# Mixer chunks by channels: weights stationary, x normalised beforehand, squares summed by tokens, the scale by a GpSimd power

## The chip, the cores and the metric

The kernel runs on one core of a Trainium2 chip. The metric is the device time of one execution in microseconds, as a median of several runs. A core has five engines that work side by side, each through its own queue in order: TensorE (PE; its weight loads are shown as PEld), VectorE (DVE), ScalarE (ACT), GpSimd (POOL) and SyncE (SP), whose queue issues almost all DMAs here. Matmuls write PSUM, a small memory of banks of 128 partitions by 512 float32; everything else lies in SBUF.

## What is computed

Two layers over 256 tokens of 1024 channels, float32. Each layer is a half-step SwiGLU FFN, a token mixer, and another half-step FFN, every one between two RMS norms:

```python
for i in range(DEPTH):
    f = swiglu_ffn(rmsnorm(x, ffn1_norm_pre[i]), ffn1_w_in[i], ffn1_w_out[i])
    x = x + 0.5 * rmsnorm(f, ffn1_norm_post[i])

    h = rmsnorm(x, mix_norm_pre[i])
    p = h @ mix_w_in[i]
    qkv, z, beta_logit, a_logit, glu_in, gates = jnp.split(p, SPLITS, axis=-1)
    y_a = gated_deltanet(qkv, z, beta_logit, a_logit, ...)
    y_b = conformer_conv(glu_in, ...)
    g_a, g_b = jnp.split(jax.nn.sigmoid(gates), 2, axis=-1)
    y = (g_a * y_a + g_b * y_b) @ mix_w_out[i]
    x = x + rmsnorm(y, mix_norm_post[i])

    f = swiglu_ffn(rmsnorm(x, ffn2_norm_pre[i]), ffn2_w_in[i], ffn2_w_out[i])
    x = x + 0.5 * rmsnorm(f, ffn2_norm_post[i])
```

`gated_deltanet` runs a causal convolution of 4 taps and SiLU over q, k and v, makes q and k of unit length per head (8 heads of 128), forms decays from a cumulative sum, inverts a lower triangular matrix for each chunk of 64 tokens and scans over the chunks. `conformer_conv` gates half of its 2048 inputs by the sigmoid of the other half, runs a causal convolution of 31 taps per channel, a layer norm, SiLU and a projection.

## The kernel before

**Tiles.** The tokens are two blocks of 128 (`tb` 0 and 1). Every large product is done in three matmuls (`mm3`, lines 366 to 369): x and the weights are each split into a rounded part `hi` and the rest `lo`, and hi*hi, hi*lo and lo*hi are summed in PSUM. x is stationary (128 channels by 128 tokens), the weights move past it, 512 columns at a time.

**Weights.** `Stream` (lines 117 to 155) brings them in pieces of 128x1024: a DMA on SP into `raw` (three buffers), a copy on ACT into `whi` (line 146) and a subtraction into `wlo` (line 147) on DVE, or on POOL for the pieces of the mixer whose number is in the set `POOL`. `whi` and `wlo` have eight buffers each; a new piece is loaded when an old one is used up.

**Order.** PE's instructions run in the order in which the program writes them down. The other engines' order comes from a list scheduler, in which work written earlier goes first, moved by the offsets in `CFG` (`conv` back by 800, `ev` ahead by 1000 and so on). Side work that needs PE is woven in by `Lanes`: a job is a generator; `DELAY` gives the ticks from its adding to its first step and between its steps, `AFTER` the jobs that must have ended before. `tick` is called after every third of matmuls or so, 16 times in a chunk of 512 columns.

**The FFN** (`ffn`, line 446): 11 chunks of 512 columns, gated on eviction with the row scale `rstd`, transposed (line 464) and split again for the second product, whose results go through `post` (line 349): a Square with a sum on ACT, `rsqrt` (lines 237 to 256; for one column eleven small DVE instructions with the two before it), and an update of x (line 364). `pre` (line 271) then multiplies x by the norm's weights (line 277), transposes it (line 283), splits it (lines 260, 261) and computes the row scale r beside this (line 290). The scale is applied when results leave PSUM.

**The mixer** (`mixer`, line 484) runs through the 17 chunks of `PLAN` by `proj_in` (line 372). For each chunk and token block a PSUM bank (`mm`, four banks) receives tokens by 512 columns; `ev` copies it with the row scale into a staging tile (line 908). For the chunks of g, k, v and q, which are needed with channels on the partitions, `to_channels` (line 509) transposes the staging tile in blocks of 128x128 into PSUM (line 513, tag `tr`, three banks). `fin_glu` gates g; `conv4` (line 557) makes the four taps: an ACT copy with a scale (line 560), three DVE multiply-adds (line 562), SiLU on ACT. Beside this run:

- `conv31` (line 533), 31 taps over a pair of channel tiles on DVE (line 546), in one PSUM bank (`cacc`), the four pairs and the inverse one after the other
- `decays` (line 580): small DVE work on the `ka` chunk's first 16 columns, a cumulative sum on PE (lines 618 to 620), the sums out to DRAM and back as a broadcast (lines 632, 636), differences on DVE (line 639), Exp on ACT
- `k_tokens` and `q_tokens` (lines 659, 807): `squares` takes the squares of k or q on ACT (line 648), `sums` adds them over the channels by matmuls with a column of ones (line 656)
- `similarity` (matmuls on line 698), `inverse`, `merge`, and the scan
- `conv_norm` (line 975), the layer norm after the convolutions; its transposes (line 985) wait for the last of them (line 552)

Of the kernel before, what the change touches and what calls it, by code (L numbers as in the profile page):

```python
# [158 lines left out]
def trunk(ctx: ExitStack, tc: tile.TileContext, x_in, wfirst, consts, feat, pch, tokp,  # L159
# [49 lines left out]
    V.memset(ones, 1.0)  # L209
    warm = cpool.tile([P, 1], F32, name="warm")  # L210
# [46 lines left out]

    def split(hi, lo, src):

        S.copy(hi, src)  # L260
        V.tensor_tensor(lo, src, hi.bitcast(F32), op=ALU.subtract)  # L261
# [4 lines left out]

    def halves(tb):
        return [slots.tile([P, 2, 4, P], F32R, name="xt", tag=f"xt{tb}{hf}") for hf in range(2)]


    def pre(tb, wbc, xws):
        xw = slot(xws, [P, D], name="xw")
        xh = halves(tb)
        r = small(1, f"rstd{tb}")
        for hf in range(2):
            cs = slice(hf * 512, hf * 512 + 512)
            V.tensor_tensor(xw[:, cs], x[tb][:, cs], wbc[:, cs], op=ALU.mult)

        def steps():
            for hf in range(2):  # L280
                tr = ps_tr()
                for k in range(4):
                    T.transpose(tr[:, k, :], xw[:, hf * 512 + k * P: hf * 512 + (k + 1) * P], ident)
                with prio(tc, "pre"):
                    split(xh[hf][:, 0], xh[hf][:, 1], tr)
                if hf == 0:
                    yield
            with prio(tc, "stat"):
                ss = small(1, "ss")
                S.activation(xw, x[tb], AF.Square, accum_out=ss)  # L290
                V.tensor_scalar(ss, ss, 1.0 / D, RMS_EPS, op0=ALU.mult, op1=ALU.add)
                rsqrt(r, ss, 1)

        due[tb] = lanes.add(f"pre{tb}", steps())
        return xh, r


    def start():
# [14 lines left out]
        def stat(tb):  # L313
            jk = slot(15 + tb, [P, D], name="jk")
            ss = small(1, "ss")
            S.activation(jk, x[tb], AF.Square, accum_out=ss)
            V.tensor_scalar(ss, ss, 1.0 / D, RMS_EPS, op0=ALU.mult, op1=ALU.add)
            rsqrt(r[tb], ss, 1)
# [30 lines left out]
    def post(tb, acc, wbc, half, fws, jks):  # L349
        fw = slot(fws, [P, D], name="fw")  # L350
        jk = slot(jks, [P, D], name="jk")
        ss = small(2, "ss2")
        for hf in range(2):
            cs = slice(hf * 512, hf * 512 + 512)
            S.activation(jk[:, cs], acc[hf], AF.Square, accum_out=ss[:, hf:hf + 1])  # L355
            V.scalar_tensor_tensor(fw[:, cs], acc[hf], half, wbc[:, cs], op0=ALU.mult, op1=ALU.mult)  # L356
        s1 = small(1, "ss1")
        V.tensor_tensor(s1, ss[:, 0:1], ss[:, 1:2], op=ALU.add)
# [13 lines left out]
    def proj_in(xt, chunks, ev, fin, first=2):  # L372
# [111 lines left out]
    def mixer(xt, l, after_mix):  # L484
# [7 lines left out]
        rs = [xt[tb][1] for tb in range(2)]  # L492

# [3 lines left out]
        S.activation(aexp, tp[:, 0, :], AF.Exp)  # L497
# [24 lines left out]
        def fin_glu(c, stage):  # L522
            for i in range(2):
# [3 lines left out]
                tr = to_channels(stage, [i * P, 256 + i * P])  # L527
                sg = stt("sg")
                S.activation(sg, tr[:, 1, :], AF.Tanh, scale=0.5, bias=bgh[:, t:t + 1])
                S.activation(sg, sg, AF.Copy, scale=0.5, bias=0.5)  # L530
                V.scalar_tensor_tensor(h_of(t), tr[:, 0, :], pcc(C_BA, t), sg, op0=ALU.add, op1=ALU.mult)
# [48 lines left out]
        def decays():  # L580
# [10 lines left out]
            eo = small(32, "eo", bufs=1)  # L591
            S.activation(eo[:, 0:16], ba[:, 0].rearrange("p g b h -> p (g b h)"), AF.Exp, scale=-1.0)
# [32 lines left out]
            S.activation(ex, xin, AF.Exp)  # L625
            S.activation(neg_eg, ex[:, 0:16], AF.Copy, scale=-1.0)
# [6 lines left out]
            for gp in range(2):  # L633
# [7 lines left out]
                S.activation(dt, dt, AF.Exp)  # L641
                S.activation(gx[:, 4:8, :], gx[:, 4:8, :], AF.Exp)
# [3 lines left out]
        def squares(src, si):  # L646
            sq = slot(si, [P, 4, SEQ], name="sq")
            S.activation(sq, src, AF.Square)  # L648
            return sq

        def sums(sq):
            ps = ps_gd([P, 512])
            for tb in range(2):
                for hl in range(4):
                    th = tb * 4 + hl
                    T.matmul(ps[:, th:th + 1], sq[:, hl, tb * P:(tb + 1) * P], ones, start=True, stop=True)  # L656
            return ps

        def k_tokens(gp):
            sq = squares(kT[gp], 18 + gp)  # L660
            for tb in range(2):
                if tb:
                    yield
                tr = ps_tr()
                for hl in range(4):
                    T.transpose(tr[:, hl, :], kT[gp][:, hl, tb * P:(tb + 1) * P], ident)
# [3 lines left out]
            ps = sums(sq)  # L670
            V.tensor_scalar(ve, ps[:, 0:8], 1e-6, None, op0=ALU.add)
# [135 lines left out]
        def q_tokens(gp):  # L807
            sq = squares(qT[gp], 18 + gp)
            yield
            V.tensor_scalar(vq[:, gp * 8:gp * 8 + 8], sums(sq)[:, 0:8], float(P), P * 1e-6, op0=ALU.mult, op1=ALU.add)  # L810
# [79 lines left out]

        last = {}

        def ev(c, tb, ps):
            name, n = PLAN[c][0], chunks[c][0]
            if tb == 0:
# [5 lines left out]
            if kind in "gkvq":  # L901
                t = tokt("stg")
                if name == "ka":
                    S.activation(ba[:, :, :, tb, :], ps[:, 0:16].rearrange("p (k g h) -> p k g h", k=2, g=2),
                                 AF.Copy, scale=rs[tb])
                    S.activation(t[:, 0:256], ps[:, 16:272], AF.Copy, scale=rs[tb])
                else:
                    S.activation(t[:, :n], ps[:, :n], AF.Copy, scale=rs[tb])
                stage[c, tb] = t
            elif kind == "z":  # L910
                gp = int(i)
                if tb == 0:
                    z[gp] = slot(8 + gp, [P, 8, P], name="z")
                S.activation(z[gp][:, tb * 4:tb * 4 + 4, :], ps.rearrange("p (h d) -> p h d", h=4), AF.Silu,
                             scale=rs[tb])
            else:
                if tb == 0:
                    gate[name] = slot({"a0": 6, "a1": 7, "b0": 10, "b1": 11}[name], [P, 2, 512], name="gate")
                if tb not in rsh:
                    rsh[tb] = small(1, f"rsh{tb}")  # L920
                    V.tensor_scalar(rsh[tb], rs[tb], 0.5, None, op0=ALU.mult)
                S.activation(gate[name][:, tb, :], ps, AF.Tanh, scale=rsh[tb])

        rsh = {}
# [76 lines left out]
        def conv_out(tb):  # L1001
            cT[tb] = halves(1) if tb else [slot(hf, [P, 2, 4, P], F32R, name="ct") for hf in range(2)]
# [63 lines left out]
        proj_in(xt, chunks, ev, fin)  # L1066
# [71 lines left out]
    for l in range(depth):  # L1138
        ffn(list(xt), l, R_F1POST, make_pre(l, R_MPRE, 18, 15), first=2 if l else 0)
# [81 lines left out]
```

## Time and profile before

| | us |
|---|---|
| median of 3 runs | 1457.55 (1455.1 to 1458.56) |
| the profiled execution | 1458.55 |
| its span, first to last instruction | 1456.7 |
| DVE busy | 979.3 |
| ACT busy | 771.0 |
| POOL busy | 248.4 |
| PE idle at line 985, waiting for line 552 | 7.4 |

The difference of 1.85 us between the profiled execution and its span lies before the first and after the last instruction that the profile shows. Busy times of different engines overlap. The granted clock of TensorE was 0.973 of full speed on average. The first layer's FFN1 takes the time up to some 202 us, its mixer to some 557, its FFN2 to some 735; the second layer's mixer runs from some 925 to some 1270.

### The profile page before, as it was taken

What the parts mean: (1) busy time and instruction counts of PE and PEld (TensorE: products, weight loads), DVE (VectorE), ACT (ScalarE), POOL (GpSimd) and SP (SyncE); (2) the same over time, 40 slices, a digit from 0 to 9 for tenths busy, and PEclk for the clock granted to TensorE, in tenths of its full rate; (3) what the DMA queues carried; (4) which work ended last, traced back from release to release, by engine and by line L of the source; (5) the groups of instructions that cost most, each with busy time, mean ns of one, the idle gap of its engine ahead of it and who ended that gap; (6) DMA issues with size and microseconds to landing.
All of it is one profiled execution on the core that took longest, in us unless ns stands there. A gap on an engine that the chain in (4) does not pass through costs nothing.

```text
span 1456.7 us, 19518 instructions
## 1 busy us (share of the span) xinstructions
PE 1398.4 (96%) x6972; PEld 1159.0 (80%) x6972; DVE 979.3 (67%) x2103; ACT 771.0 (53%) x1206; POOL 248.4 (17%) x116
## 2 busy tenths in 40 slices
PE   8999999798998999999999999998989989999997
PEld 6788878687787887888888888787868878888886
DVE  6655477687659878655486553887876687875543
ACT  6544347657354645544355442585754554464531
POOL 0000015467340000000000000174755200000000
PEclk9999999799799999999999999997999999999999
DMA  7765545445333556655467665563543435665551
GB/s 250 226 201 181 187 167 191 154 129 173 88 130 118 193 194 197 213 180 183 146 226 216 181 184 174 175 211 115 184 136 115 132 115 199 191 209 188 187 183 57
DMA packets 82963, 250.65 MB, mean 172 GB/s; under 512 B 21136, under 2 KB 21680, under 8 KB 82864
## 3 DMA queue, kind: packets, MB, share of 16 engines
q1 hardware_dynamic: 82576, 249.32, 54.0%
q8 instruction: 55, 0.90, 0.2%
q14 instruction: 44, 0.36, 0.1%
q10 hardware_dynamic: 288, 0.07, 0.0%
HBM read 245.14 MB, written 4.21 MB: 171 GB/s over the span
## 4 chain that ended last, share of the span: by engine, by line
PE 80%; DVE 6%; DMA 5%; ACT 4%; issue 3%; POOL 2%; SPq 0%; DVEq 0%; ACTq 0%; POOLq 0%
PE mm L367 23%; PE mm L369 23%; PE mm L368 23%; DVE wlo L147 2%; POOL wlo L147 2%; ACT whi L146 2%; DMA raw<-w1i 2%; DMA raw<-mw 1%; PE gd L656 1%; PE tr L464 1%; DMA raw<-w2i 1%; PE tr L513 1%; PE gd L698 1%; PE gd L818 1%; DVE dt L639 1%
## 5 line engine op out<-in xcount | busy, mean ns | idle before, releaser
L146 ACT CAST whi<-raw 128x1024 fp32r<-128x1024 f32 (+2 forms) x445 | 462.7, 1041 | 401.6 <-PE mm L369 266.5
L147 DVE TENSOR_TENSOR wlo<-raw,whi 128x1024 fp32r<-128x1024 f32 (+2 forms) x345 | 416.4, 1209 | 269.3 <-ACT whi L146 263.5
L367 PE MATMUL mm<-whi,xt 128*128 128x512 f32 (+2 forms) x1280 | 513.7, 401 | 1.2 <-ACT whi L146 0.9
L369 PE MATMUL mm<-whi,xt 128*128 128x512 f32 (+2 forms) x1280 | 499.6, 390 | 2.3 <-DVE xt L261 2.3
L368 PE MATMUL mm<-wlo,xt 128*128 128x512 f32 (+2 forms) x1280 | 498.7, 390 | 1.0 <-DVE wlo L147 1.0
L369 PEld LDWEIGHTS mm<-whi,xt 128*128 128x128 f32 x1280 | 243.5, 190 | 56.3 <-DVE xt L261 6.0
L367 PEld LDWEIGHTS mm<-whi,xt 128*128 128x128 f32 x1280 | 244.7, 191 | 45.8 <-ACT whi L146 1.3
L368 PEld LDWEIGHTS mm<-wlo,xt 128*128 128x128 f32 x1280 | 244.6, 191 | 45.9 <-DVE wlo L147 2.4
L147 POOL TENSOR_TENSOR wlo<-raw,whi 128x1024 fp32r<-128x1024 f32 x100 | 239.0, 2403 | 228.6 <-ACT whi L146 196.2
L546 DVE SCALAR_TENSOR_TENSOR cacc<-hT,pc,cacc 128x254 f32<-128x254 f32 (+28 forms) x464 | 186.8, 469 | 25.3 <-ACT cacc L542 25.3
L367 PE MATMUL mm<-whi,act 128*128 128x512 f32 x352 | 137.6, 391 | 0.0
L369 PE MATMUL mm<-whi,act 128*128 128x512 f32 x352 | 137.1, 389 | 0.0
L368 PE MATMUL mm<-wlo,act 128*128 128x512 f32 x352 | 137.0, 389 | 0.0
L691 POOL MEMSET u<- 128x1024 f32 x4 | 3.8, 958 | 675.6 <-ACT jk L355 652.6
L562 DVE SCALAR_TENSOR_TENSOR c<-tr,pc,c 128x255 f32<-128x255 f32 (+1 forms) x144 | 67.1, 477 | 22.1 <-ACT c L560 21.9
L369 PEld LDWEIGHTS mm<-whi,act 128*128 128x128 f32 x352 | 66.1, 188 | 13.8
L367 PEld LDWEIGHTS mm<-whi,act 128*128 128x128 f32 x352 | 66.1, 188 | 13.5
L368 PEld LDWEIGHTS mm<-wlo,act 128*128 128x128 f32 x352 | 66.1, 188 | 13.5
L452 ACT ACTIVATE ag<-mm,rstd 128x256 f32<-128x256 f32 x88 | 41.0, 474 | 40.0 <-DVE ag L453 23.8
L453 DVE SCALAR_TENSOR_TENSOR ag<-mm,rstd,ag 128x256 f32<-128x256 f32 x88 | 41.5, 480 | 18.0 <-ACT ag L452 18.0
L356 DVE SCALAR_TENSOR_TENSOR fw<-mm,wbc 128x512 f32<-128x512 f32 x24 | 16.0, 689 | 46.8 <-ACT jk L355 46.8
L656 PE MATMUL gd<-ones,sq 128*128 128x1 f32 x128 | 25.1, 326 | 20.5 <-ACT sq L648 14.8
(232 smaller groups left out, 1281.5 us busy)
## 6 DMA issues: line engine op xcount, KB each, us to landing
raw<-mw SPq DMA_DIRECT2D x168, 512.0 KB, 3.4
raw<-w1i SPq DMA_DIRECT2D x88, 512.0 KB, 4.3
raw<-w2i SPq DMA_DIRECT2D x88, 512.0 KB, 4.2
raw<-w1o SPq DMA_DIRECT2D x44, 512.0 KB, 3.7
raw<-w2o SPq DMA_DIRECT2D x44, 512.0 KB, 3.4
wbc<-feat SPq DMA_DIRECT2D x13, 512.0 KB, 4.8
raw<-mkb SPq DMA_DIRECT2D x8, 272.0 KB, 3.0
xs<-x SPq DMA_DIRECT2D x4, 512.0 KB, 3.9
```

The lines of the kernel that those rows point to most:

```text
L146: nc.scalar.copy(hi[:, c], raw[:, c])
L147: eng.tensor_tensor(lo[:, c], raw[:, c], hi.bitcast(F32)[:, c], op=ALU.subtract)
L356: V.scalar_tensor_tensor(fw[:, cs], acc[hf], half, wbc[:, cs], op0=ALU.mult, op1=ALU.mult)
L367: T.matmul(o, xh, wh, start=start, stop=False)
L368: T.matmul(o, xh, wl, start=False, stop=False)
L369: T.matmul(o, xl, wh, start=False, stop=stop)
L452: S.activation(a[:, 0, :], ps[:, 0:256], AF.Silu, scale=xt[tb][1])
L453: V.scalar_tensor_tensor(a[:, 1, :], ps[:, 256:512], xt[tb][1], a[:, 0, :], op0=ALU.mult, op1=ALU.mult)
L464: T.transpose(tr[:, k, tb, :], a[:, 1, k * P:(k + 1) * P], ident)
L546: cur = V.scalar_tensor_tensor(accs[i][:, sh:], h_of(t)[:, :SEQ - sh], dw(t, KW - 1 - sh), accs[i][:, sh:], op0=ALU.mult, op1=ALU.add)
L562: V.scalar_tensor_tensor(acc[:, sh:], src[:, :SEQ - sh], cw(t, 3 - sh), acc[:, sh:], op0=ALU.mult, op1=ALU.add)
L656: T.matmul(ps[:, th:th + 1], sq[:, hl, tb * P:(tb + 1) * P], ones, start=True, stop=True)
```

## The change

Five things are changed together.

1. **By channels.** For the chunks g1, kb, g2, g3, v1, v0, q0 and q1 (`by_ch`) the weights are stationary, in blocks of 128x128, and x moves, 256 tokens at once. The result has channels on the partitions, two blocks of 256 tokens to a PSUM bank. `ev` makes no copy; `conv4` and `fin_glu` read that bank, which stays taken until they have. g0, k1 and ka are done as before. Both token blocks of x lie in one tile (`joint`).
2. **Normalised x.** Before the mixer `pre` computes the row scale first and multiplies x by it (`norm=True`), so that evictions in the mixer need none.
3. **The row scale.** `rms_scale` is one DVE instruction and a GpSimd power to -0.5 in place of `rsqrt`; the division by 1024 goes into the Square's scale. The `rsqrt` of eight or sixteen columns and that of `conv_norm` stay.
4. **Squares by tokens.** `by_tokens` transposes k or q, squares on ACT from PSUM and reduces on DVE. `squares` and `sums` are gone. For k the transposes were there already.
5. **Times.** `DELAY`, `CFG` and `POOL` have new numbers (POOL has 56 pieces a layer in place of 50), and two Exp of `decays` stand at other places.

```diff
 DELAY = {
-    "first": (1, 2), "ffn": (6,), "pre0": (14, 3), "pre1": (15, 2), "yt0": (8, 3), "yt1": (8, 2),
-    "f_g0": (4, 2), "f_g1": (7, 5), "c0": (8,), "f_k1": (3, 4), "f_ka": (10, 2), "decays": (6, 23),
-    "kt1": (26, 2), "sim1": (30, 2), "f_kb": (3, 2), "kt0": (20, 2), "sim0": (18, 7), "inv": (25,),
+    "first": (1, 2), "ffn": (14, 1), "pre0": (11, 4, 4), "pre1": (14, 2, 2), "yt0": (9, 3, 8), "yt1": (13, 3),
+    "f_g0": (0, 0), "f_g1": (8, 9), "c0": (9,), "f_k1": (8, 0), "f_ka": (20, 2, 2), "decays": (6, 25),
+    "kt1": (26, 10), "sim1": (25, 5, 0), "f_kb": (3, 0, 2), "kt0": (18, 2, 2), "sim0": (18, 7), "inv": (25,),
...
-POOL = {3, *range(16, 64), 67}
-CFG = dict(stat=0, conv=-800, ev=1000, tok=4, st=4, post=300, pre=100, fin=None, tokens=200)
+POOL = {2, 3, 5, 9, *range(15, 54), *range(55, 65), 67, 68, 88}
+CFG = dict(stat=0, conv=-800, ev=300, tok=4, st=4, post=50, pre=100, fin=None, tokens=0)
...
+    def rms_scale(o, ms, more=None):
+        V.tensor_scalar(ms, ms, RMS_EPS if more is None else more, None if more is None else RMS_EPS,
+                        op0=ALU.add, **({} if more is None else dict(op1=ALU.add)))
+        nc.gpsimd.tensor_tensor(o, ms, mhalf, op=ALU.pow)
...
+        def stat():
+            ss = small(1, "ss")
+            S.activation(xw, x[tb], AF.Square, scale=D ** -0.5, accum_out=ss)
+            rms_scale(r, ss)
+        if norm:
+            stat()
...
+            if norm:
+                V.scalar_tensor_tensor(xw[:, cs], x[tb][:, cs], r, wbc[:, cs], op0=ALU.mult, op1=ALU.mult)
...
+        def piece_ch(c, i, ps, w):
+            n, kp = chunks[c]
+            for k in range(kp):
+                kt = i * kp + k
+                xh, xl = (xj[kt // 4][:, :, j, kt % 4, :] for j in range(2))
+                for b in range(n // P):
+                    o = ps[b // 2].rearrange("p (g b t) -> p g b t", g=2, b=2)[:, b % 2]
+                    wh, wl = (w[j][:, k * n + b * P:k * n + (b + 1) * P] for j in range(2))
+                    T.matmul(o, wh, xh, start=kt == 0 and b % 2 == 0, stop=False)
+                    T.matmul(o, wh, xl, start=False, stop=False)
+                    T.matmul(o, wl, xh, start=False, stop=kt == 7 and b % 2 == 1)
+                    if b % 2:
+                        lanes.tick()
...
+            if c in by_ch:
+                ps = [ps_mm() for _ in range(chunks[c][0] // (2 * P))]
+                for i in range(8 // chunks[c][1]):
+                    piece_ch(c, i, ps, st.peek(0))
+                    st.done()
+                with prio(tc, "ev"):
+                    ev(c, None, ps)
+                fin(c)
+                continue
...
+        def by_tokens(src, tb, sq, ss):
+            tr = ps_tr()
+            for hl in range(4):
+                T.transpose(tr[:, hl, :], src[:, hl, tb * P:(tb + 1) * P], ident)
+            t = slice(tb * 4, tb * 4 + 4)
+            S.activation(sq[:, t, :], tr, AF.Square)
+            V.tensor_reduce(ss[:, t], sq[:, t, :], axis=mybir.AxisListType.X, op=ALU.add)
+            return tr
...
+            if tb is None:
+                stage[c] = {j: t[:, k * SEQ:(k + 1) * SEQ] for j, (t, k) in
+                            enumerate((t, k) for t in ps for k in range(2))}
```

More of the change, by code (lines that the diff above doesn't have):

```diff
@@ L264, in trunk, with joint, halves_of, pre @@
     due = [None, None]
+    def joint():
+        return [slots.tile([P, 2, 2, 4, P], F32R, name="xt", tag=f"xt{hf}") for hf in range(2)]
+    cur = [None]
+    def halves_of(t):
+        return [t[:, i] for i in range(2)]
     def halves(tb):
-        return [slots.tile([P, 2, 4, P], F32R, name="xt", tag=f"xt{tb}{hf}") for hf in range(2)]
-    def pre(tb, wbc, xws):
+        if tb == 0:
+            cur[0] = joint()
+        return [t[:, tb] for t in cur[0]]
+    def pre(tb, wbc, xws, norm):
         xw = slot(xws, [P, D], name="xw")
@@ L287, in steps @@
                     yield
[L288 to L292, printed above, removed]
+            if not norm:
+                with prio(tc, "stat"):
+                    stat()
         due[tb] = lanes.add(f"pre{tb}", steps())
@@ L315, in stat @@
             ss = small(1, "ss")
-            S.activation(jk, x[tb], AF.Square, accum_out=ss)
-            V.tensor_scalar(ss, ss, 1.0 / D, RMS_EPS, op0=ALU.mult, op1=ALU.add)
-            rsqrt(r[tb], ss, 1)
+            S.activation(jk, x[tb], AF.Square, scale=D ** -0.5, accum_out=ss)
+            rms_scale(r[tb], ss)
         order = ExitStack()
@@ L354, in post @@
             cs = slice(hf * 512, hf * 512 + 512)
-            S.activation(jk[:, cs], acc[hf], AF.Square, accum_out=ss[:, hf:hf + 1])
+            S.activation(jk[:, cs], acc[hf], AF.Square, scale=D ** -0.5, accum_out=ss[:, hf:hf + 1])
             V.scalar_tensor_tensor(fw[:, cs], acc[hf], half, wbc[:, cs], op0=ALU.mult, op1=ALU.mult)
-        s1 = small(1, "ss1")
-        V.tensor_tensor(s1, ss[:, 0:1], ss[:, 1:2], op=ALU.add)
-        V.tensor_scalar(s1, s1, 1.0 / D, RMS_EPS, op0=ALU.mult, op1=ALU.add)
         r = small(1, "rpost")
-        rsqrt(r, s1, 1)
+        rms_scale(r, ss[:, 0:1], ss[:, 1:2])
         for hf in range(2):
@@ L369, in mm3, with proj_in @@
         T.matmul(o, xl, wh, start=False, stop=stop)
-    def proj_in(xt, chunks, ev, fin, first=2):
+    def proj_in(xt, chunks, ev, fin, first=2, by_ch=(), xj=None):
         def piece(c, tb, i, ps, w):
@@ L526, in fin_glu @@
                 t = 2 * c + i
-                tr = to_channels(stage, [i * P, 256 + i * P])
+                if isinstance(staged, dict):
+                    a, g = staged[i], staged[2 + i]
+                else:
+                    tr = to_channels(staged, [i * P, 256 + i * P])
+                    a, g = tr[:, 0, :], tr[:, 1, :]
                 sg = stt("sg")
-                S.activation(sg, tr[:, 1, :], AF.Tanh, scale=0.5, bias=bgh[:, t:t + 1])
+                S.activation(sg, g, AF.Tanh, scale=0.5, bias=bgh[:, t:t + 1])
                 S.activation(sg, sg, AF.Copy, scale=0.5, bias=0.5)
-                V.scalar_tensor_tensor(h_of(t), tr[:, 0, :], pcc(C_BA, t), sg, op0=ALU.add, op1=ALU.mult)
+                V.scalar_tensor_tensor(h_of(t), a, pcc(C_BA, t), sg, op0=ALU.add, op1=ALU.mult)
         def conv31(pair):
@@ L591, in decays @@
             eo = small(32, "eo", bufs=1)
+            S.activation(aexp, tp[:, 0, :], AF.Exp)
             S.activation(eo[:, 0:16], ba[:, 0].rearrange("p g b h -> p (g b h)"), AF.Exp, scale=-1.0)
@@ L641, in decays @@
                 S.activation(dt, dt, AF.Exp)
+                if gp == 0:
+                    S.activation(ex, xin, AF.Exp)
+                    S.activation(neg_eg, ex[:, 0:16], AF.Copy, scale=-1.0)
                 S.activation(gx[:, 4:8, :], gx[:, 4:8, :], AF.Exp)
                 DT[gp], GX[gp] = dt, gx
[L646 to L657, printed above, removed]
+        def by_tokens(src, tb, sq, ss):
[6 more added lines that the diff above has]
+            return tr
         def k_tokens(gp):
-            sq = squares(kT[gp], 18 + gp)
+            sq = slot(18 + gp, [P, 8, P], name="sq")
+            ss = small(8, "ssk")
             for tb in range(2):
@@ L663, in k_tokens @@
                     yield
-                tr = ps_tr()
-                for hl in range(4):
-                    T.transpose(tr[:, hl, :], kT[gp][:, hl, tb * P:(tb + 1) * P], ident)
+                tr = by_tokens(kT[gp], tb, sq, ss)
                 S.copy(ktok[gp][:, tb * 4:tb * 4 + 4, :], tr)
@@ L669, in k_tokens @@
             ve, rk = small(8, "ve"), small(8, "rk")
-            ps = sums(sq)
-            V.tensor_scalar(ve, ps[:, 0:8], 1e-6, None, op0=ALU.add)
+            ps = ps_gd([P, 512])
+            V.tensor_scalar(ve, ss, 1e-6, None, op0=ALU.add)
             hv, t8 = ps[:, 8:16], ps[:, 24:32]
@@ L807, in q_tokens @@
         def q_tokens(gp):
-            sq = squares(qT[gp], 18 + gp)
+            sq = slot(18 + gp, [P, 8, P], name="sq")
+            ss = small(8, "ssk")
+            by_tokens(qT[gp], 0, sq, ss)
             yield
-            V.tensor_scalar(vq[:, gp * 8:gp * 8 + 8], sums(sq)[:, 0:8], float(P), P * 1e-6, op0=ALU.mult, op1=ALU.add)
+            by_tokens(qT[gp], 1, sq, ss)
+            V.tensor_scalar(vq[:, gp * 8:gp * 8 + 8], ss, float(P), P * 1e-6, op0=ALU.mult, op1=ALU.add)
             qk = slot(18 + gp, [P, 8, P], name="qk")
@@ L889, in mixer @@
         chunks = [{"ka": (272, 2), "kb": (256, 4)}.get(name, (512, 2)) for name, _ in PLAN]
+        by_ch = {c for c, (name, _) in enumerate(PLAN) if c > 1 and name[0] in "gkvq" and name != "ka"}
         last = {}
@@ L894, in ev @@
             name, n = PLAN[c][0], chunks[c][0]
-            if tb == 0:
+            if not tb:
                 for job in BEFORE.get(name, ()):
@@ L918, in ev @@
                     gate[name] = slot({"a0": 6, "a1": 7, "b0": 10, "b1": 11}[name], [P, 2, 512], name="gate")
[L919 to L924, printed above, removed]
+                S.activation(gate[name][:, tb, :], ps, AF.Tanh, scale=0.5)
         def heads(staged, n, which):
@@ L929, in heads @@
                     yield
-                tr = to_channels(staged, [(b + i) * P for i in range(2)])
+                tr = None if isinstance(staged, dict) else to_channels(staged, [(b + i) * P for i in range(2)])
                 for i in range(2):
-                    which(b + i, tr[:, i, :])
+                    which(b + i, staged[b + i] if tr is None else tr[:, i, :])
         def take(c):
             name = PLAN[c][0]
-            kind, staged = name[0], [stage.pop((c, tb)) for tb in range(2)]
+            kind = name[0]
+            staged = stage.pop(c) if c in by_ch else [stage.pop((c, tb)) for tb in range(2)]
             if kind == "g":
@@ L1001, in conv_out @@
         def conv_out(tb):
-            cT[tb] = halves(1) if tb else [slot(hf, [P, 2, 4, P], F32R, name="ct") for hf in range(2)]
+            cT[tb] = halves_of(joint()[0]) if tb else [slot(hf, [P, 2, 4, P], F32R, name="ct") for hf in range(2)]
             for hf in range(2):
@@ L1132, in f @@
                 hold["w"] = load_feat(l, r, ws)
-            xt[tb] = pre(tb, hold["w"], xws + tb)
+            xt[tb] = pre(tb, hold["w"], xws + tb, norm)
         return f
```

29 lines of the change are left out of this document (13 added, 16 removed), and 9 rows, old and new, of the table DELAY.

## The prediction

> **What bounds the kernel now.** I read the page first: the span, the busy time of each engine, then the groups, the waits of PE, and PE's timeline for the pace of single instructions.
>
> ```profile
> span 1456.7 us, 19518 instructions
> PE 1398.4 (96%) x6972; PEld 1159.0 (80%) x6972; DVE 979.3 (67%) x2103; ACT 771.0 (53%) x1206; POOL 248.4 (17%) x116
> ```
>
> PE is busy nearly all the time and the other engines are not, so PE's one queue sets the end. But its busy time is not all matmul at full pace. The profiled execution took 1458.55 us, 1.85 us around its span, and 1.0 us more than the median of the three runs, 1457.55. I make the sum against the span and shift it at the end.
>
> A matmul's shown duration is its passage through the pipeline; the cost is the distance from one start to the next. In the timeline of PE (start, duration, line, shape) I take two starts of L368 39 matmuls apart in an undisturbed stretch of 512 columns, then two of L369 33 apart in chunk kb, 256 columns wide, and the weight loads' row.
>
> ```profile
> 190.12 0.39 PE L368 MATMUL mm<-wlo,act 128*128 128x512 f32 x1
> ...
> 198.96 0.39 PE L368 MATMUL mm<-wlo,act 128*128 128x512 f32 x1
> ```
> ```profile
> 247.84 0.28 PE L369 MATMUL mm<-whi,xt 128*128 128x256 f32 x1
> ...
> 251.80 0.28 PE L369 MATMUL mm<-whi,xt 128*128 128x256 f32 x1
> ```
> ```profile
> L367 PEld LDWEIGHTS mm<-whi,xt 128*128 128x128 f32 x1280 | 244.7, 191 | 45.8 <-ACT whi L146 1.3 <-ACT xt L260 0.8
> ```
>
> 8.84 us / 39 = 0.2267 us for 512 columns; 3.96 / 33 = 0.120 us for 256. Every matmul here has its own weight load and the 0.19 us of it shown do not pace the 0.120.
>
> Next, what PE does between matmuls: the timeline around a group of four transposes, the group of L656, and PE's waits (us in total, times, longest).
>
> ```profile
> 223.91 0.39 PE L369 MATMUL mm<-whi,xt 128*128 128x512 f32 x1
> 224.15 0.60 PE L513 MATMUL tr<-cst,stg 128*128 128x128 f32 x4
> 224.50 0.48 PE L367 MATMUL mm<-whi,xt 128*128 128x512 f32 x1
> 224.82 0.40 PE L368 MATMUL mm<-wlo,xt 128*128 128x512 f32 x1
> ```
> ```profile
> L656 PE MATMUL gd<-ones,sq 128*128 128x1 f32 x128 | 25.1, 326 | 20.5 <-ACT sq L648 14.8 <-ACT cacc L542 5.0 <-ACT kt L667 0.7
> ```
> ```profile
> PE gd L656 <- ACT sq L648: 14.8, 4, 4.7
> PE tr L985 <- DVE hT L552: 7.4, 2, 3.7
> PE gd L698 <- DVE dt L639: 6.8, 2, 4.8
> ...
> PE mm L369 <- DVE xt L261: 2.3, 5, 0.6
> ```
>
> From 223.91 to 224.82 are 0.91 us for two matmuls and four transposes; two steps of 0.2267 taken off leave 0.457, or 0.114 us a transpose. L656, the matmuls that sum squares against a column of ones, is dear: 25.1 us of work for one output column each, and 20.5 us in which PE stood before them, mostly for the Square on ACT. What stands behind PE there is the next chunk's matmuls, so both are on the path. The granted clock (PEclk) falls around those places:
>
> ```profile
> 264.00:300.00 36.00, 26.75 (x125) 0.72 0.32 106
> 360.00:390.00 30.00, 22.73 (x98) 0.72 0.32 88
> 985.00:1020.00 35.00, 29.98 (x148) 0.76 0.37 114
> 1075.00:1105.00 30.00, 22.45 (x102) 0.77 0.35 93
> ```
> ```profile
> 284.58 0.63 PE L368 MATMUL mm<-wlo,xt 128*128 128x512 f32 x1
> 285.00 0.63 PE L369 MATMUL mm<-whi,xt 128*128 128x512 f32 x1
> ```
>
> The last two starts lie 0.42 us apart instead of 0.227: right after L656 a matmul runs at about half pace.
>
> **The change, part by part.**
>
> *Sums of squares (L656) go.* k_tokens and q_tokens now transpose to tokens and let ACT square and DVE reduce, so no PE instruction waits for ACT's Square. Gone: 25.1 + 20.5 = **-45.6 us**. q_tokens gains 8 transposes for each of its four calls (k had its own already): 32 x 0.114 = **+3.7**. The reductions, 8 a layer over 128x512, have no row; on DVE I put them at some 0.65 us each, like the 512-wide products of L277 below, and off the path, since DVE has idle time there (169 us busy of 231, below). If that cover were gone they would cost 5 us a layer.
>
> *By channels.* Eight chunks a layer (g1, kb, g2, g3, v1, v0, q0, q1) no longer pass L513: 8+4+8+8 and four times 8 transposes, 60 a layer, 120 in all, 120 x 0.114 = **-13.7**. Chunk kb keeps 48 matmuls of 256 columns. The other seven turn 48 matmuls of 512 into 96 of 256: 11.52 for 10.88 us, +0.64 each, 14 of them, **+9.0**. The moving operand is now two runs of 128 columns, which no row shows; I take kb's pace, and keep the 0.19 us load as the other end (below). ACT's staging copies go too, at no gain: ACT is not the bound.
>
> The Trainium skill ("TensorE: Matmul & The Clock Gate", Part 2, Back-to-back issue gap) gives N/2.4 + 2.5 ns as the distance, an estimate of 109 ns at 256 and 216 at 512. By that the pair would lose 2.6 ns instead of 13 and the +9.0 would be 1.7; the rows here say 120 and 227, and the measurement decides.
>
> *Clock.* Those four windows hold 36x0.28, 30x0.28, 35x0.24 and 30x0.23 us of lost clock; taking the clock as either whole or half there, as the pair at 284 suggests, that is twice as long at half, 67.6 us. The idle time and work of L656 (45.6) and the 6.8 of L698 explain 52.4; the other 15.2 us of work ran at half, 7.6 us lost. I take **-7**, between 0 (the wait at L698 keeps it cold) and -12 (L698 and the scan warm up too).
>
> *rms_scale.* Eleven small DVE instructions become one and a POOL power. At the very end nothing covers them:
>
> ```profile
> 1449.85 0.15 DVE L358 TENSOR_TENSOR ss<-ss 128x1 f32<-128x1 f32 x1
> ...
> 1452.02 0.21 DVE L249 TENSOR_SCALAR rpost<-nw_a,nw_y 128x1 f32<-128x1 f32 x1
> ```
> ```profile
> L681 POOL TENSOR_TENSOR kt<-kt,kds 128x512 f32<-128x512 f32 x4 | 4.2, 1044 | 10.1 <-DVE kds L679 7.7 <-DVE nw_y L256 2.5
> ...
> L1213 POOL MEMSET const-float32-0.0<- 128x1 f32 x1 | 0.1, 104 | 0.2 <-issue 0.2
> ```
>
> 2.4 us now. The power is not in the trace: between 0.1 (one element, no reading) and 1.04 (512 elements). Nearer the former in size; 0.5, with 0.15 before it and 0.2 for two handings-over, 0.85: **-1.5** (-0.9 to -2.0).
>
> *Boundary FFN1 to mixer.* x is now normalised before it is split, so a Square, an add and a power stand on the chain of each token block. What they stand on, and DVE beside POOL there:
>
> ```profile
> 191.42 0.15 DVE L358 TENSOR_TENSOR ss<-ss 128x1 f32<-128x1 f32 x1
> ...
> 196.62 0.21 DVE L249 TENSOR_SCALAR rpost<-nw_a,nw_y 128x1 f32<-128x1 f32 x1
> ...
> 198.20 3.49 DVE L277 TENSOR_TENSOR xw<-x,wbc 128x512 f32<-128x512 f32 x2
> ...
> 212.55 1.28 DVE L277 TENSOR_TENSOR xw<-x,wbc 128x512 f32<-128x512 f32 x2
> ```
> ```profile
> 198.43 2.71 POOL L147 TENSOR_TENSOR wlo<-raw,whi 128x1024 fp32r<-128x1024 f32 x1 [6.64 <-ACT whi L146]
> ```
> ```profile
> L290 ACT ACTIVATE xw<-x 128x1024 f32<-128x1024 f32 x10 | 10.8, 1082 | 0.0
> ```
>
> The old scale took 5.4 us with weight splits between its steps; the new takes about 0.9, and the second statistic adds 1.1 + 0.2 + 0.9. The chain gets some 2 us shorter, but PE waits only 2.3 us at all L369 places, so little can be won. Against it: POOL now also splits pieces 2, 5 and 9 in this stretch, 2.4 us each. A power stands in POOL's queue behind such a split, the DVE update of x (L364) behind the power, the weight splits behind that on DVE, and PE behind those. The rows show the second cost: the two products of L277 took 1.28 us at 212 and 3.49 at 198, in the time of POOL's split: 2.2 us lost. I take **+1** (-3 to 6 x 2.4 = +14). The later POOL pieces have the cover of eight pieces in the ring.
>
> The Trainium skill ("SBUF — State Buffer", section SBUF: two separate sides) says that a GpSimd instruction and a DVE one with two SBUF inputs hold the shared ports for their whole time, the loser waiting. That speaks against moving splits to POOL, and the row at 198 agrees. With every one of the twelve added splits (six a layer) on the path, the sum by that rule alone would be an estimated 29 us higher, 1438; where the rows bear it out, at the boundary, it is a rival below.
>
> *Joint x tiles, the later transposes of FFN (DELAY 14 for 6), aexp moved:* no cost; each is needed a chunk or more later. Pieces keep their order on SP; the DMAs of decays, similarity and inverse move with their steps, behind raw loads as now.
>
> *New waits.* By channels, each chunk keeps two of the four PSUM banks until its convolution has read them, and PE's first matmul of the chunk after next waits for that. ACT and DVE need:
>
> ```profile
> L562 DVE SCALAR_TENSOR_TENSOR c<-tr,pc,c 128x255 f32<-128x255 f32 (+1 forms) x144 | 67.1, 477 | 22.1 <-ACT c L560 21.9
> ```
>
> Twelve of 0.477 are 5.7 us, and about 2 more for the first ACT copy; the next chunk covers 11.5. During the inverse DVE shares its time, so some holds run over: **+6** (0 to +30).
>
> Sum: -45.6 + 3.7 - 13.7 + 9.0 - 7 - 1.5 + 1 + 6 = -48.1; span 1408.6; with 1.85 around it and 1.0 less for the median, 1409.5. **Forecast 1410 us.** I leave the waits at L985 and L698 as they are.
>
> **The rivals.**
>
> *Decays' round trip becomes the wait.*
>
> ```profile
> 267.66 0.29 PE L618 MATMUL gd<-g,cst 128*128 128x16 f32 x2
> ...
> 290.40 3.78 PE L698 MATMUL gd<-kT 128*128 128x128 f32 x16 [4.77 <-DVE dt L639]
> ```
>
> From the cumulative sum to the matmuls of similarity pass 22.7 us, with the DMA of the sums out to DRAM, its broadcast back and the DVE work of L639 among them. The stalls for L656 that go were inside it. If the trip stays as long, PE waits at L698 or for a transpose's buffer instead: up to 10 us a layer, 1430. Against: sim1 comes some 10 ticks later (kt1, which it follows, ends 41 ticks after ka where it ended at 32), and the row copy no longer stands behind an Exp.
>
> *The convolutions on DVE become the bound.* L985 waits for the last of them already.
>
> ```profile
> 228.00:459.00 231.00, 210.26 (x1259) 178.31 (x1258) 169.24 (x529) 138.07 (x255) 119.48 (x53) 0.92 0.45 144
> ```
> ```profile
> DVE cacc L546 <- ACT cacc L542: 25.3, 2, 12.7
> DVE ve L671 <- PE gd L656: 14.5, 4, 5.9
> DVE vq L810 <- PE gd L656: 13.7, 4, 4.3
> ```
>
> DVE works 169 of these 231 us. With 25 fewer it would be at 82%. But its own waits for L656, 14 us a layer, go too, and 12.7 wait for an ACT instruction in the wrong place. If only the 14 us are won, some 8 of 24 us a layer come back as waiting at L985: 1425.
>
> *POOL at the boundary:* all six splits on the path, 1424.
>
> *Better:* no new waits and both old ones (14 us) re-timed away, 1390.
>
> *Slower: PSUM holds.* If every one of the 14 full chunks holds its banks 16 us (DVE giving each second slot to other work and starting late), PE waits 4.5 us each, +63: 1473. It decides from 11.5 us of hold; the gain is gone at about 15.
>
> *Slower: the load paces 256 columns in the new layout.* 0.19 for 0.12 us, 14 x 96 x 0.07 = 94: 1504. Chunk kb speaks against it.
>
> **How the numbers follow.** Forecast 0.45; decays 0.14; DVE 0.15; POOL 0.07; better 0.07; PSUM 0.09; load 0.03. Range 1388 to 1440: it takes in the faster rivals and leaves out the last two and the outer ends of others. Of the faster cases I count 0.03 as ending within 0.2% (about what a measurement of this kernel tells from no change), with several rivals at once: faster 0.85, same 0.03, slower 0.12.
>
> **What would show it.** In the new profile: no sums against ones, the clock near 1 where the four windows had 0.72 to 0.77, L513 with a quarter of its instructions, 256-column matmuls 0.120 us apart. Wrong would be: PE waits on the first matmul of a by-channel chunk (PSUM), at similarity (decays), at L985's successor over 5 us (DVE), or starts 0.19 us apart.

## The result and the profile after

The changed kernel takes 1409.24 us (median of 4 runs, 1407.66 to 1415.26); the kernel before takes 1457.62 beside it. The ratio is 0.968, with a 95% interval of 0.965 to 0.971, or some 47 us. The forecast was 1410. The profiled execution took 1408.11 us.

The page after: its span, the busy time of each engine, and the granted clock of TensorE in 40 slices of the span (in tenths):

```profile
span 1406.0 us, 20213 instructions
PE 1362.3 (97%) x7428; PEld 1157.0 (82%) x7428; DVE 945.5 (67%) x1876; ACT 748.8 (53%) x1182; POOL 294.5 (21%) x152
PEclk9999999999999999999999999998999999999999
```

The span fell by 50.7 us. Of this 36.1 are busy time of PE (1398.4 to 1362.3) and 14.6 are time in which it stood (58.3 to 43.7). PE's waits after, to be held against those shown of before:

```profile
PE gd L744 <- ACT kt L713: 7.8, 4, 2.8
PE tr L700 <- ACT qT L613: 6.0, 4, 2.6
PE tr L313 <- DVE xw L305: 4.4, 2, 2.2
PE tr L333 <- DMA cst<-consts: 4.3, 1, 4.3
PE tr L700 <- ACT kt L713: 3.6, 2, 1.8
PE gd L744 <- DVE at L747: 3.5, 2, 2.0
PE mm L392 <- DVE ss L263: 2.6, 3, 1.1
PE mm L416 <- ACT sg L578: 1.6, 1, 1.6
```

L700 are the transposes that replace the sums, L744 is similarity (L698 before), L313 the transposes of normalised x, L416 the first matmul of a by-channel step. The wait at the layer norm (7.4 us at L985 before) is gone. At L744 PE waits 11.3 us, at L700 some 10.

In the program the tiles named `tr` and `gd` share the three `tr` banks, and similarity's matmuls read nothing but k. So what they wait for is a bank, whether the profile names ACT's copies (kt), `at` or, in the kernel before, the differences of `decays` (dt). In the changed kernel the first of them start at 273.58 us, while the differences (L687) run from 275.02 to 279.24.

The by-channel matmuls, in PE's timeline: two starts of L418 ten steps of three apart, and the group of L416 with that of its weight loads (busy us, mean ns, idle time of the engine before them and what ended it).

```profile
258.16 0.28 PE L418 MATMUL mm<-xt,wlo 128*128 128x256 f32 x1
...
261.76 0.28 PE L418 MATMUL mm<-xt,wlo 128*128 128x256 f32 x1
```
```profile
L416 PE MATMUL mm<-xt,whi 128*128 128x256 f32 x480 | 139.8, 291 | 1.6 <-ACT sg L578 1.6
...
L416 PEld LDWEIGHTS mm<-xt,whi 128*128 128x128 f32 x480 | 93.9, 196 | 2.1 <-ACT sg L578 2.0
```

3.60 us / 30 = 0.120 us, as in chunk kb before: a moving operand in two runs costs no more, and the load of 0.196 us does not pace it.

Where the time went by stage, from one first Square of `post` to the next (line 355 before, 382 after):

| stage | before | after |
|---|---|---|
| start to the end of the first FFN1 | 189.4 | 185.5 |
| first mixer | 345.3 | 316.1 |
| FFN2 | 187.8 | 188.1 |
| second layer's FFN1 | 187.8 | 188.5 |
| second mixer | 339.0 | 320.1 |
| last FFN2 | 187.7 | 189.5 |

The mixers gave 48 us. Whether the parts gave it one by one, as the prediction's sum has it, is the question of the experiments.

### The profile page after: what moved, and what is told of

Read it like the earlier page. It is cut to its first block, busy times and chain, and to the rows that moved or that the text cites. A ratio compares the mean times of both kernels' runs of the same rounds, so it can differ in the third digit from the quotient of the medians.

```text
span 1406.0 us, 20213 instructions
## 1 busy us (share of the span) xinstructions
PE 1362.3 (97%) x7428; PEld 1157.0 (82%) x7428; DVE 945.5 (67%) x1876; ACT 748.8 (53%) x1182; POOL 294.5 (21%) x152
## 4 chain that ended last, share of the span: by engine, by line
PE 84%; DVE 8%; DMA 3%; ACT 2%; issue 2%; POOL 1%; DVEq 0%; POOLq 0%; ACTq 0%; SPq 0%
PE mm L391 22%; PE mm L393 22%; PE mm L392 22%; PE mm L416 3%; PE mm L417 3%; PE mm L418 3%; DVE wlo L148 2%; PE tr L512 1%; DMA raw<-w2i 1%; DMA raw<-mw 1%; DVE cacc L595 1%; DVE dt L687 1%; DMA gx<-gd 1%; DVE iup L773 1%; DVE iu L771 1%
## 5 line engine op out<-in xcount | busy, mean ns | idle before, releaser
L148 DVE TENSOR_TENSOR wlo<-raw,whi 128x1024 fp32r<-128x1024 f32 (+1 forms) x333 | 407.7, 1228 | 290.8 <-ACT whi L147 285.8
L391 PE MATMUL mm<-whi,xt 128*128 128x512 f32 (+1 forms) x1024 | 410.0, 400 | 0.9 <-ACT whi L147 0.9
L392 PE MATMUL mm<-wlo,xt 128*128 128x512 f32 (+1 forms) x1024 | 398.8, 389 | 3.1 <-DVE ss L263 2.6
L393 PE MATMUL mm<-whi,xt 128*128 128x512 f32 (+1 forms) x1024 | 399.4, 390 | 0.4 <-DVE xt L270 0.4
L148 POOL TENSOR_TENSOR wlo<-raw,whi 128x1024 fp32r<-128x1024 f32 (+1 forms) x112 | 266.7, 2393 | 323.7 <-ACT whi L147 303.8
L393 PEld LDWEIGHTS mm<-whi,xt 128*128 128x128 f32 x1024 | 193.5, 189 | 41.8 <-DVE xt L270 1.1
L392 PEld LDWEIGHTS mm<-wlo,xt 128*128 128x128 f32 x1024 | 194.2, 190 | 40.4 <-DVE wlo L148 5.0
L391 PEld LDWEIGHTS mm<-whi,xt 128*128 128x128 f32 x1024 | 194.3, 190 | 37.5 <-ACT whi L147 1.3
L416 PE MATMUL mm<-xt,whi 128*128 128x256 f32 x480 | 139.8, 291 | 1.6 <-ACT sg L578 1.6
L417 PE MATMUL mm<-xt,whi 128*128 128x256 f32 x480 | 137.4, 286 | 0.0
L418 PE MATMUL mm<-xt,wlo 128*128 128x256 f32 x480 | 137.3, 286 | 0.0
L393 PE MATMUL mm<-whi,act 128*128 128x512 f32 x352 | 137.2, 390 | 0.0
L392 PE MATMUL mm<-wlo,act 128*128 128x512 f32 x352 | 137.0, 389 | 0.0
L416 PEld LDWEIGHTS mm<-xt,whi 128*128 128x128 f32 x480 | 93.9, 196 | 2.1 <-ACT sg L578 2.0
L417 PEld LDWEIGHTS mm<-xt,whi 128*128 128x128 f32 x480 | 93.8, 195 | 0.1
L418 PEld LDWEIGHTS mm<-xt,wlo 128*128 128x128 f32 x480 | 93.7, 195 | 0.0
L393 PEld LDWEIGHTS mm<-whi,act 128*128 128x128 f32 x352 | 66.1, 188 | 14.0
L391 PEld LDWEIGHTS mm<-whi,act 128*128 128x128 f32 x352 | 66.1, 188 | 13.5
```

The source lines that it names most:

```text
L148: eng.tensor_tensor(lo[:, c], raw[:, c], hi.bitcast(F32)[:, c], op=ALU.subtract)
L391: T.matmul(o, xh, wh, start=start, stop=False)
L392: T.matmul(o, xh, wl, start=False, stop=False)
L393: T.matmul(o, xl, wh, start=False, stop=stop)
L416: T.matmul(o, wh, xh, start=kt == 0 and b % 2 == 0, stop=False)
L417: T.matmul(o, wh, xl, start=False, stop=False)
```

## The experiments

Two theories. The ledger: PE's work and waits add up term by term, so that each part is worth its term. The rival: PE's waits depend on what else is in PE's queue and in the three `tr` banks at that moment, so that one part cashes in what another makes possible. Twelve kernels were run: some take a part out of the changed kernel, some add a part to the one before, and some change only the times at which side work is put into PE's queue. Each ratio is to the kernel before, run beside the experiment (medians of 1455.7 to 1457.3 us).

**The old sums put back.** `k_tokens`, `q_tokens`, `squares` and `sums` as before, in the changed kernel.

```diff
-                tr = by_tokens(kT[gp], tb, sq, ss)
...
+            ps = sums(sq)
```

> The changed kernel with the old sums of squares (squares on ACT, 64 calls of matmuls with a column of ones) put back in k_tokens and q_tokens, all else as changed. Ledger theory (PE's own work and the waits in front of it set the time, term by term): the old matmuls return with 25 us of work and up to 20 us of waiting, the q transposes go (3.7): 1409 + 25 to 42, so 1434 to 1451, with the granted clock down again to 0.7 to 0.8 around them. Rival, the new times of the side work did it: the sums hide, under 1420.

Measured: 1442.47 us, ratio to before 0.991 (0.989 to 0.993); against 0.968 that is 33 us lost, inside the ledger's range, and the granted clock is 0.72 to 0.80 around the sums again. The parts are less like the ledger. PE stands 33.6 us in front of the sums, where the kernel before had 20.5:

```profile
PE gd L707 <- ACT sq L699: 25.2, 2, 12.6
PE gd L707 <- ACT kt L718: 8.4, 4, 2.3
```

Two waits of 12.6 us for q's Square make most of it; before, no wait for a Square was longer than 4.7 us. Against that, the 10 us at the transposes and 6.5 of those at similarity are gone. The times are those of the changed kernel, placed for other work, so the 33 us are not the price of the old sums alone.

**No chunk by channels.**

```diff
-        by_ch = {c for c, (name, _) in enumerate(PLAN) if c > 1 and name[0] in "gkvq" and name != "ka"}
+        by_ch = set()
```

> The changed kernel with no chunk by channels (by_ch empty): all chunks go with x stationary through staging tiles and L513's transposes as before; normalised x, the new sums, scale and times stay. Ledger theory: the transposes come back (+13.7), the 256-wide matmuls go (-9.0), the small PSUM wait goes (-1.6): 1409 + 3, so 1407 to 1418. Rival, by-channel layout is what the gain hangs on (it frees ACT, DVE and the tr banks so that waits vanish): 1425 or more.

Measured: 1424.94 us, 0.978 (0.976 to 0.981), 15 us lost, where the ledger had 3 (9 at most) and the rival 16 or more: at the edge of the rival. PE's busy time rises by 7.9 us to 1370.2, so there the gain was sized too low, and it stands 10 us longer. The new waits are those of the staging transposes (L558) for a `tr` bank:

```profile
PE tr L558 <- DVE dt L687: 10.3, 2, 5.9
...
PE tr L558 <- DVE hT L580: 4.4, 2, 2.2
```

L558 needs nothing from the differences of `decays` (dt). It waits because `decays` holds one of the three banks until they are done. By channels there is no L558 in that place.

**The new sums alone, on the kernel before.**

```diff
-            sq = squares(kT[gp], 18 + gp)
+            sq = slot(18 + gp, [P, 8, P], name="sq")
...
+                tr = by_tokens(kT[gp], tb, sq, ss)
```

> The kernel before with the new sums of squares alone (by_tokens in k_tokens and q_tokens), old times and chunks. Ledger theory: 45.6 us of L656 and its waits go, 3.7 come, up to 7 of slow clock go: 1457 - 42 to - 49 if nothing new waits. Rival, other waits take their place without the new times (decays' round trip before similarity, the last convolution before the layer norm, up to 10 us a layer each): 1425 to 1440.

Measured: 1451.41 us, 0.997 (0.996 to 0.9985): 4 us won where the ledger had 42 or more and even the rival 17. PE's busy time fell by 21.1 us (to 1377.3), but its idle time rose from 58.3 to 72.3:

```profile
PE gd L693 <- DVE dt L639: 15.9, 2, 8.1
PE tr L649 <- ACT qT L564: 11.2, 6, 2.8
PE tr L983 <- DVE hT L552: 9.6, 2, 4.8
PE tr L649 <- ACT kt L662: 6.6, 2, 3.3
```

The differences cost 6.8 before and 15.9 now. PE came earlier to jobs that were not ready earlier: the old sums had covered part of the round trip of `decays`, which has hardly become shorter. From the cumulative sum to the last difference it takes 22.7 and 18.0 us in the two layers of the kernel before, and 20.2 and 17.7 here.

**The old times in the changed kernel**, and then the old `DELAY` alone, and the old `CFG` and `POOL` alone.

```diff
-DELAY = {"first": (1, 2), "ffn": (14, 1), "pre0": (11, 4, 4), ...}
+DELAY = {"first": (1, 2), "ffn": (6,), "pre0": (14, 3), ...}
-POOL = {2, 3, 5, 9, *range(15, 54), *range(55, 65), 67, 68, 88}
+POOL = {3, *range(16, 64), 67}
-CFG = dict(stat=0, conv=-800, ev=300, tok=4, st=4, post=50, pre=100, fin=None, tokens=0)
+CFG = dict(stat=0, conv=-800, ev=1000, tok=4, st=4, post=300, pre=100, fin=None, tokens=200)
```

> The changed kernel with DELAY, CFG and POOL of before; what is computed and how is as changed. Ledger theory: PE's work is the same, only waits move: 1409 + 0 to 12. Rival, the new times are the main part: 1430 or more, with new waits of PE at similarity, layer norm or the first matmuls of by-channel chunks.

> The changed kernel with the old DELAY alone (new CFG and POOL). If the places of PE's side work make up the 38 us that the old times cost: 1435 to 1450, with PE's waits at L700 and similarity back at 30 us and more. If the priorities and POOL's pieces do: 1405 to 1420.

> The changed kernel with the old CFG and POOL alone (new DELAY). The reverse of the run before: 1405 to 1420 if the places of PE's side work are what counts, 1430 or more if priorities and POOL's pieces are. If POOL's splits at the boundary cost what was feared (14 us at most), this one would even be a little faster than the changed kernel: 1395 to 1405.

Measured: all old 1447.55 us, 0.994 (0.993 to 0.996); old `DELAY` alone 1445.63, 0.992 (0.991 to 0.994); old `CFG` and `POOL` alone 1405.03, 0.9645 (0.963 to 0.966). So the places of PE's side work are worth 36 us in the changed kernel, and priorities and POOL's pieces nothing that shows; the interval of the last overlaps that of the changed kernel, and whether it is faster stays open. With the old `DELAY` PE waits again at similarity, at the transposes and, newly, for PSUM:

```profile
PE gd L743 <- DVE dt L686: 10.1, 2, 5.7
PE tr L699 <- ACT qT L612: 9.3, 8, 3.2
PE mm L415 <- DVE c L610: 9.0, 4, 3.4
```

The last line is the PSUM hold of the prediction: chunks' banks that are not read in time. With the new places it is 1.6 us.

**The new times alone, on the kernel before.** The same three tables, the other way round.

> The kernel before with DELAY, CFG and POOL of the changed one and nothing else. If the new times are a gain by themselves: 1456 - 20 or more, below 1436. If they only let the new sums and the by-channel chunks cash in (interaction): 1448 to 1462, with PE still standing at the sums against ones for the Square, as in the run of the changed kernel with the old sums (25 us there).

Measured: 1459.91 us, 1.002 (1.0005 to 1.003). By themselves the times win nothing. In front of the sums PE stands 12.8 us, less than the 20.5 before and far from the expected 25, and other waits eat that up:

```profile
PE tr L284 <- DVE xw L278: 16.7, 9, 4.2
PE tr L514 <- DVE dt L640: 11.8, 2, 6.3
PE gd L657 <- ACT sq L649: 9.3, 2, 4.7
```

L514 are the staging transposes, which wait for the bank of `decays`. L284 are the transposes of x after `pre`, at which PE waits 1.0 us in the kernel before. The new times put them earlier (`pre0` has 11 ticks in place of 14) and `post` less far ahead (50 in place of 300), and with `rsqrt` x is not ready there. Which of the two counts more was not run. So the places are right only for the work that is now there, the faster scale included.

**The new sums with the times of their own jobs, on the kernel before.**

```diff
-"decays": (6, 23), "kt1": (26, 2), "sim1": (30, 2), "qt0": (22, 3, 6, 3), ...
+"decays": (6, 25), "kt1": (26, 10), "sim1": (25, 5, 0), "qt0": (19, 2, 6, 11, 13), ...
```

> The kernel before with the new sums and of the new times only those of the k, q, decays and similarity jobs (DELAY of decays, kt0, kt1, sim0, sim1, qt0, qt1, qs, f_ka, f_kb, f_k1, f_q0, f_q1). The new sums alone gave 4 us, since PE then stood 16 us for the decay differences, 22 at the new transposes and 10 at the layer norm. If those places are what holds the gain back: 1420 to 1435, with the wait for the differences under 6 us. If the by-channel chunks are needed for it (fewer users of the three tr banks, no staging): 1440 to 1452.

Measured: 1446.94 us, 0.992 (0.991 to 0.994), some 10 us won: in the range of the second expectation. The wait for the differences left similarity and went to the staging transposes (L505 here), the first place behind it that needs a `tr` bank:

```profile
PE tr L505 <- DVE dt L631: 12.9, 2, 7.4
PE gd L685 <- ACT kt L654: 12.3, 4, 4.7
PE tr L975 <- DVE hT L544: 9.6, 2, 4.8
```

That the by-channel chunks are what this kernel lacks is shown only in part. The changed kernel without them has the wait for the differences too (10.3 us), yet it takes 1424.94 us: some 20 us between the two come from other parts of the change. This kernel also keeps the two Exp of `decays` at their old places. From the cumulative sum to the last difference it takes 19.2 and 16.9 us; the changed kernel takes 13.8 and 13.5, and without by-channel chunks 16.2 and 14.6. What the moved Exps are worth alone was not run.

**The power.** `rsqrt` on DVE put back into `rms_scale` of the changed kernel, and the power alone given to the kernel before, at all three places in the program where the row scale is made.

```diff
-        nc.gpsimd.tensor_tensor(o, ms, mhalf, op=ALU.pow)
+        rsqrt(o, ms, 1)
```

> The changed kernel with DVE's shift and three Newton steps (rsqrt) in place of the GpSimd power in rms_scale; the add before it stays. Ledger theory: the end gets longer by 1.3 (0.8 to 1.9) and the two chains before each mixer by up to 1.5 each, little elsewhere: 1409 + 1 to 8. Rival, the power waits in POOL's queue and costs as much as it saves: 1405 to 1410.

> The kernel before with rms_scale (the GpSimd power) in place of rsqrt for single columns, and nothing else; the scale is still applied at evictions. Ledger theory, the prediction's term: 1.5 us at the end, up to 3 at the block boundaries where PE waits for x: 1457 - 2 to - 5. If the power by itself is worth the 24 us that its removal cost in the changed kernel: 1435 or less; if that worth exists only together with normalised x and the new post and pre times, the first holds.

Measured: 1432.8 us, 0.983 (0.982 to 0.985), 22 us lost; and 1455.67, 0.999 (0.998 to 1.0005), less than the 2 to 5 us expected and nothing that shows. Both expectations of the first fall short: the place is right, the size not. In it PE waits 26.7 us for x at its transposes, normalised before the mixers (L305) and not normalised before the FFNs (L307); in the changed kernel it waits 4.4 us there:

```profile
PE tr L313 <- DVE xw L305: 18.9, 4, 7.9
PE tr L313 <- DVE xw L307: 7.8, 6, 1.9
```

At L305, where x is normalised, two scales stand one behind the other on the chain. DVE's timeline at the first such place, of the changed kernel with `rsqrt` and then of the changed kernel itself:

```profile
187.48 0.20 DVE L263 TENSOR_SCALAR ss<-ss 128x1 f32<-128x1 f32 x1
...
191.79 3.17 DVE L388 SCALAR_TENSOR_TENSOR x<-fw,rpost,x 128x512 f32<-128x512 f32 x2
196.17 0.15 DVE L263 TENSOR_SCALAR ss<-ss 128x1 f32<-128x1 f32 x1 [1.21 <-ACT xw L297]
...
198.29 2.29 DVE L148 TENSOR_TENSOR wlo<-raw,whi 128x1024 fp32r<-128x1024 f32 x1
200.50 1.41 DVE L305 SCALAR_TENSOR_TENSOR xw<-x,rstd,wbc 128x512 f32<-128x512 f32 x2
```
```profile
187.52 0.20 DVE L263 TENSOR_SCALAR ss<-ss 128x1 f32<-128x1 f32 x1
188.43 1.41 DVE L388 SCALAR_TENSOR_TENSOR x<-fw,rpost,x 128x512 f32<-128x512 f32 x2 [0.71 <-POOL rpost L265]
...
192.04 0.15 DVE L263 TENSOR_SCALAR ss<-ss 128x1 f32<-128x1 f32 x1
192.85 3.49 DVE L305 SCALAR_TENSOR_TENSOR xw<-x,rstd,wbc 128x512 f32<-128x512 f32 x2 [0.66 <-POOL rstd L265]
```

The first scale takes 4.3 us by `rsqrt`, since splits of weights get between its steps, and 0.9 by the power; the second 2.1 and 0.8 before the split that follows. In the kernel before the second scale stood beside the chain and PE waited only 1.0 us for x, so there the power has nothing to win.

Normalised x is not the whole reason. With the new times and `rsqrt` the kernel before waits 16.7 us at L284 for an x that is not normalised, 9.5 of them before the two mixers. Here it is 26.7 us, 18.9 of them before the mixers. So, by comparing these two kernels, the larger part of the wait belongs to the new times with the slow scale, and some 9 us to normalised x with its second scale. No run takes the two apart: `rsqrt` with normalised x and the old times was not tried.

**FFN transposes later, on the kernel before.**

```diff
-    "first": (1, 2), "ffn": (6,), "pre0": (14, 3), "pre1": (15, 2), "yt0": (8, 3), "yt1": (8, 2),
+    "first": (1, 2), "ffn": (14, 1), "pre0": (14, 3), "pre1": (15, 2), "yt0": (8, 3), "yt1": (8, 2),
```

> The kernel before with the FFN's transposes 14 ticks after their chunk in place of 6, nothing else. In the profile of before PE waits 2.7 us for the gated tile at L464 and loses some 4 at those places in the first FFN, and the profile of the changed kernel has none of it: 1457 - 2 to - 5. If that loss only moves to the start of the second product: 1455 to 1458.

Measured: 1451.94 us, 0.9965 (0.995 to 0.998), 5 us won. The wait of 2.7 us at L464 is gone.

**Four jobs later still.** From the kernel with the old `CFG` and `POOL`.

```diff
-"sim0": (18, 7), "kt1": (26, 10), "qt0": (19, 2, 6, 11, 13), "qt1": (17, 5, 7),
+"sim0": (28, 7), "kt1": (26, 12), "qt0": (22, 2, 6, 11, 13), "qt1": (20, 5, 7),
```

> The changed kernel with the old CFG and POOL (1405 before) and four jobs later: sim0 first due 28 ticks after kb (18), kt1's second step 12 ticks on (10), qt0 and qt1 due 3 ticks later. The waits at similarity for ACT's copies (12.5) and at q's transposes for the SiLU (7.1) should shrink: 1395 to 1403 if nothing else moves; 1403 to 1412 if the wait only moves to the next job.

Measured: 1410.9 us, 0.968 (0.966 to 0.969), no gain over the 0.9645 of the kernel that it starts from: the second expectation. Similarity's wait for ACT's copies fell from 12.5 to 5.4 us and 9.7 came, which end with a scale of DVE (`kds`):

```profile
PE gd L735 <- DVE kds L716: 9.7, 2, 4.8
PE tr L691 <- ACT qT L604: 9.6, 6, 3.2
PE gd L735 <- ACT kt L704: 5.4, 2, 2.7
```

## Why the prediction was right, and where its steps were not

The total came out within 1 us. Of its two halves the waits and the end agree, -15.0 forecast and -14.6 measured, and PE's work fell 3 us more than forecast, by 36.1 for 33.1 (25.1 of L656, transposes, 256-wide matmuls, clock).

That the waits agree so closely is luck in part. Some 10 us that the sum had left alone went (7.4 at the layer norm, 2.7 at L464), 13.5 that it did not have came (10.2 at the new transposes, 3.3 at similarity), and the 6 for PSUM were 1.6. Above all, the sum has no term for the new `DELAY`, which keeps such waits away: taken back in the changed kernel, it costs 36 us. The terms one by one:

- *L656's work* (-25.1): right. The group is gone, and the new sums alone took 21.1 us off PE's busy time.
- *L656's waits* (-20.5): right as part of this change, wrong as a term of their own. Alone the new sums won 4 us, because the wait moved to the differences, the transposes and the layer norm. This is the rival called decays' round trip, and it happened in that run. In the changed kernel it does not happen; with the old `DELAY` (10.1 us) or without by-channel chunks (10.3 us) the wait for the differences is there. The prediction's reason against this rival, that similarity comes later, is not what the trace shows: in the first layer similarity starts 8.1 us after the cumulative sum, where it was 22.7 before. It does not need the differences to start, only a bank, and the trip itself is shorter (13.8 us for 22.7).
- *By channels* (-13.7 + 9.0): the pace of 0.120 us held to the digit. The term was too small: taking it out cost 15 us, since it also keeps PE's transposes out of the three banks. The prediction had put the missing staging down as no gain. The 2.6 ns that it estimates for a pair of matmuls come to 2.5 by its own formula; the 1.7 us stand.
- *New waits* (+6 for PSUM): 1.6 measured. The mechanism is real, with the old `DELAY` such waits are 9.0 and 3.6 us.
- *L985 and L698 left as they are:* neither stayed. 7.4 us at the layer norm went, and similarity has 11.3 for 8.0 (6.8 and 1.2).
- *The power at the end* (-1.5): 2.4 us are now 0.93.

```profile
1400.73 0.20 DVE L263 TENSOR_SCALAR ss<-ss 128x1 f32<-128x1 f32 x1
1401.66 1.41 DVE L388 SCALAR_TENSOR_TENSOR x<-fw,rpost,x 128x512 f32<-128x512 f32 x2 [0.73 <-POOL rpost L265]
```

- *The boundary* (+1): PE's waits from FFN1 to the mixer are 4.4 us after (L313) and 2.1 before, so +2.3; with the other boundaries (L392 for ss, L393 for xt) 7.4 and 3.5. The products beside POOL's split cost what the prediction priced: L305 takes 3.49 us there, 1.41 without. That `rsqrt` at the new times would have cost 22 us was not seen.
- *FFN's later transposes* at no cost: a gain of 5 on the kernel before.
- *Clock* (-7): no slice of the page but one is under 9 tenths now. Around the new transposes of k and q the clock is better than the 0.72 to 0.77 of before, but near 1 at one place of four: 0.96 from 255 to 300 us, 0.86 from 335 to 360, 0.83 from 950 to 990 and 0.86 from 1030 to 1055. Its own share of the 36.1 was not measured apart.

Errors of some 5 to 10 us each thus offset one another. The experiments refute the ledger as a rule: taken out one at a time, the sums, the by-channel chunks, the power and the times cost 33, 15, 22 and 38 us, 108 together for a gain of 47; added one at a time to the kernel before, sums, times, power and FFN's delay give 4, -3, 1 and 5. Not tried: the by-channel chunks and normalised x alone on the kernel before, the new times there together with the power, and which single entries of `DELAY` do most.

## What to carry to other kernels

A wait in front of the bounding engine is won only if what it waits for gets ready earlier, or if other work is put in its place; count its work as gain, and its idle time only with a schedule that fills it. A scarce buffer, here three PSUM banks, couples jobs that share no data: PE stands at the next instruction that needs a bank, and the profile names the holder's last reader as what ended the wait, so look whether the waiting instruction reads that tile at all. A slower chain is free only until something moves onto the path behind it, so price a replacement where it will stand and at the time at which it will be asked for, not where it stood.

## What the runs showed of the hardware

The GpSimd power of one element per partition takes 0.55 us undisturbed, the update behind it starts 0.93 us after the add began, and its mean is 0.77:

```profile
1401.08 0.55 POOL L265 TENSOR_TENSOR rpost<-ss,mhalf 128x1 f32<-128x1 f32 x1 [10.33 <-DVE ss L263]
```
```profile
L265 POOL TENSOR_TENSOR rpost<-ss,mhalf 128x1 f32<-128x1 f32 x12 | 9.3, 774 | 393.3 <-DVE ss L263 393.3
```
